# Transformer encoder layer on one core: the order of the ramp in front of the first Strassen products

## The chip, the cores and the metric

The kernel runs on one core of one Trainium2 chip. The core has five engines with instruction queues of their own: TensorE (PE, matrix products into the PSUM banks), VectorE (DVE), ScalarE (ACT), GpSimd (POOL, here for small fills and for issuing DMAs) and SyncE (SP, which issues most DMAs). Each engine runs its queue in order and waits on semaphores of the others. The metric is the device time of one run in microseconds (us); lower is better.

## What is computed

One layer of a bidirectional encoder with SEQ 1024 tokens and D_MODEL 2048, all in float32. Cut to what matters here:

```python
mod = jax.nn.silu(c) @ w_ada + b_ada
shift, scale, gate = jnp.split(mod, 3, axis=-1)
h = rmsnorm(x, pre_g) * (1.0 + scale[:, None]) + shift[:, None]
proj = h @ w_in                       # 2048 -> 4608
q, k, v, gate_a, u, gate_p = jnp.split(proj, SPLIT_POINTS, axis=-1)
y_a = windowed_gqa(q, k, v, rel_table, sink) * jax.nn.silu(gate_a)
y_p = multiscale_pool(u, w_pool_grp, pool_scale) * jax.nn.silu(gate_p)
g = jax.nn.sigmoid(h @ w_merge + b_merge)          # 2048 -> 4096
merged = g_a * (y_a @ w_br_attn) + g_p * (y_p @ w_br_pool)
out = x + gate[:, None] * rmsnorm(merged @ w_out, post_g)
```

## The kernel before

Every float32 product is made of three products of rounded halves (hi·hi, hi·lo, lo·hi): `split` writes the hi part on ACT and the lo part on DVE. The large products run through a Strassen variant with seven products per pair of 128 output rows (`strassen`; its operands of the tokens are named B11, B21, B12/T3, T2, T4, T1, B22, its accumulators X, Z, V). Seven such products of one pair are 42 matmuls of 128x512 where two groups of token tiles (j = 0, 1) take part.

Before Strassen can start, h must exist, transposed: x is loaded in rows, turned on PE, normalised, scaled and shifted. That stage is called the ramp here; all the rest of the kernel follows it and is not touched by the change but in three places named below. In the ramp:

- The first eight output pairs ("ramp pairs", numbers 0 to 7) are computed in two halves of the contraction, tiles 0 to 3 first (j = 0, 1), with their partial sums parked in DRAM (`ramp_d`). Pairs 0 to 3 run their first half as plain products (`plain_block(i, blk, j)`, 6 matmuls of 128x512 each) on x that is turned but not yet normalised, and only scaled by the modulation's scale (`raw_operands`). Pairs 4 to 7 run their first half as Strassen products on the real h. Then come tiles 4 to 7 for all eight (`SECOND`, in the order 4, 5, 6, 7, 0, 1, 2, 3), adding the parked sums (`load_parts`).
- The norm factor of a token (`rstd`) needs the sum of squares of its whole row (`square_of`, `norm_row`: 32 instructions, half on ACT, half on DVE). `factors` makes rstd, `spread_factors` turns it with a matmul (tile RB) into `rb`, the factors along the free dimension. A plain block is right only after it is multiplied by rb. `put_by(i, blk, known)` takes a block out of PSUM: with known it multiplies by rb and stores to ramp_d; without it, it copies the block to a tile `c` of the pool `ev`. These tiles are multiplied later in place and then stored (`scale_evicted`).
- `row_sums` and its helpers compute scale and shift of the modulation as matmuls with a one-column vector (GEMV) and turn the result into columns `modc` (matmul PM, then DVE). `warm(n)` issues matmuls whose result nobody reads.
- `fill_two` makes the Strassen operands of tiles 0 to 3 from the turned x: it applies shift and scale, forms the sums T3, T2, T4, T1 and splits each into hi and lo. `first_given(n)` prepares the first three weight operands of pair 4, `fill_last` the operand B22.
- The pool `ev` has 9 tiles of 128x512; the pool `big` has 56 slots and hands them out again in the order in which they come free; `xa` has 5 tiles, `wp` holds the weights ("raw" and "wide", 4 tiles).

`keep(...)` fixes the order of an instruction on its engine as it is written; instructions without it (most of `strassen`, and the parts of pairs 4 on) are placed by the scheduler. PE's order in the ramp is thus the written order. In order, the ramp before: pairs 0 and 1 up to all four blocks evicted unscaled (eight tiles of `ev`), pair 2 wholly, `factors`, `spread_factors`, the four scaled evictions of pair 2, pair 3 with the turns of tiles 4 to 7, the shift's GEMV and `fill_two` between its blocks, and the first Strassen pair.

Of the kernel before, what the change touches and what calls it, by code (L numbers as in the profile page):

```python
# [43 lines left out]
def encoder_layer(ctx: ExitStack, tc: tile.TileContext, x, c, table, w_ada, b_ada, pre_g,  # L44
# [320 lines left out]
    rows = ev.tile([P, 512], F32, tag="ev", name="rows")[0:104, 0:P]  # L365
    for r0, src in ((0, c[0]), (16, b_ada[0, 0:D]), (32, b_ada[0, D:2 * D]),
                    (48, pre_g[0]), (64, b_merge[0]), (96, pool_scale[0])):
        n = src.shape[0] // P
        nc.scalar.dma_start(rows[r0:r0 + n, :], src.rearrange("(r p) -> r p", p=P))
# [63 lines left out]
    rb = [slot("rb", F32) for _ in range(2)]  # L433

    def claim_tile(t):
        nc.gpsimd.memset(t[:, 0:1], 0.0)
# [7 lines left out]
    def spread_factors():  # L444
        for s, tag in enumerate(SEEDED):
# [5 lines left out]
            keep(nc.scalar.activation(rb[s], ps, AF.Copy))  # L451
# [196 lines left out]
    def raw_operands(j, s):  # L648

        for kh, name in enumerate(("B11", "B21") if s == 0 else ("B12", "B22")):  # L650
            src, a = xT[2 * j + kh, s], modc[:, 1, kh, j:j + 1]
# [4 lines left out]
    def scale_turned(j):  # L656

        for kh in range(2):
            for s in range(2):
                keep(nc.vector.tensor_tensor(xT[2 * j + kh, s], xT[2 * j + kh, s], rb[s], ALU.mult))  # L660
# [4 lines left out]
    def fill_two(then):  # L665

        b = {j: [[xT[2 * j + kh, s] for s in range(2)] for kh in range(2)] for j in range(2)}
        t2 = {}

        def shifted(kh, s):  # L670
            for j in range(2):
                keep(modulate(nc.scalar, b[j][kh][s], 2 * j + kh))

        shifted(0, 0)
        for j in range(2):
            pin_put("B11", j, b[j][0][0])
        shifted(0, 1)
        shifted(1, 1)
        then(0)
        for j in range(2):  # L680
            t2[j] = rp.tile([P, 512], F32, tag="tf", name=uid("tf"), bufs=2)
            keep(sub(b[j][0][1], b[j][0][1], b[j][0][0]))
            keep(sub(t2[j], b[j][1][1], b[j][0][1]))
            keep(sub(b[j][0][0], t2[j], b[j][0][0]))
            pin_put("T3", j, b[j][0][0])
        then(1)
        for j in range(2):
            pin_put("T2", j, t2[j])
        shifted(1, 0)
        for j in range(2):  # L690
            pin_put("B21", j, b[j][1][0])
        then(2)
        for j in range(2):
            keep(sub(b[j][1][0], b[j][1][0], t2[j]))
            pin_put("T4", j, b[j][1][0])
        for j in range(2):
            pin_put("T1", j, b[j][0][1])

    def fill_last():

        for j in range(2):
            hi, lo = op["B22"][j]
            keep(nc.scalar.activation(hi, xT[2 * j + 1, 1], AF.Copy))
            keep(sub(lo, xT[2 * j + 1, 1], f32(hi)))
# [29 lines left out]
    for j in range(2):  # L734
        claim(j, ("B11", "B21", "B22"))
        right[j] = slot("B12h"), slot("B12l")
        for t in right[j]:
            claim_tile(f32(t))
    for t in rb:
        claim_tile(t)  # L740
# [10 lines left out]
    for j in range(2):  # L751
        claim(j, ("T3", "T2", "T4", "T1"))
    ramp_raws(4, (0, 1))
    ramp_raws(5, (0, 1))
    ada2 = [ada_tile(2, q) for q in range(5)]
    ada2 = [at[:, kk] for at in ada2 for kk in range(2)] + ada_slots(2, range(10, KT))
# [11 lines left out]
    opened, evicted = {}, {}  # L768
# [13 lines left out]
    def put_by(i, blk, known):  # L782

        t = ev.tile([P, 512], F32, tag="ev", name=uid("c"))
        if known:
            keep(nc.vector.tensor_tensor(t, opened.pop((i, blk)), rb[int(blk[1]) - 1], ALU.mult))  # L786
# [19 lines left out]
    for step in g[:4]:  # L806
        step()
        warm(2)
    g[4]()
    turn_part(0, (0, 1), SEEDED)  # L810
    for k in range(2):
        take_turned(0, k, k == 1)
    wide_weights(0, 0)
    warm(4)
    raw_operands(0, 0)
    plain_block(0, "11", 0, "sc")
    plain_block(0, "21", 0, "sc")
    turn_part(1, (0, 1), ("at", "at"))
    for k in range(2):
        take_turned(1, k, k == 1)  # L820
    raw_operands(0, 1)
# [9 lines left out]
    for si in range(4):  # L831
        square_of(si, 0, si % 2 == 1)
    plain_block(1, "11", 0, SEEDED[0])
    plain_block(1, "21", 0, SEEDED[1])
    g = row_sums(scz, scales[1], partial(scale_columns, 1), 2)
    for step in g[:4]:
        step()
        warm(2)
    for si in range(4, 8):
        square_of(si, 0, si % 2 == 1)  # L840
    g[4]()
    warm(4)
    wide_weights(0, 1)
    raw_operands(1, 0)
    plain_block(0, "11", 1)
    put_by(0, "11", False)
    plain_block(0, "21", 1)
    put_by(0, "21", False)
    raw_operands(1, 1)
    wide_weights(1, 1)  # L850
    plain_block(0, "12", 1)
    put_by(0, "12", False)
    norm_row(0)
    plain_block(0, "22", 1)
    put_by(0, "22", False)
    wide_weights(2, 0)
    plain_block(1, "11", 1)
    put_by(1, "11", False)
    norm_row(1)
    plain_block(1, "21", 1)  # L860
    put_by(1, "21", False)
    for n, blk in enumerate(("12", "22")):
        plain_block(1, blk, 0, "mm")
        plain_block(1, blk, 1)
        put_by(1, blk, False)
        norm_row(2 + n)
    wide_weights(2, 1)
    for n, blk in enumerate(BLOCKS):
# [1042 lines left out]
```

## Time and profile before

| | |
|---|---|
| median of 3 runs | 2143.91 us (2141.66 to 2144.96) |
| profiled execution: its time / its span | 2146.2 us / 2144.4 us |
| PE busy | 2086.1 us (97%) |
| DVE busy | 1556.2 us (73%) |
| ACT busy | 1117.0 us (52%) |
| DMA, mean over the span | 222 GB/s |
| granted TensorE clock, mean | 0.992 |

The profile comes from one execution on the chip. "Busy" counts the time with an instruction of that engine under way; an idle stretch is put down to what ended it. A row of the timeline gives start and length in us, the engine, the line of the kernel, the operation, output<-input and, in brackets, how long the engine had been idle and who released it. PE issues matmuls back to back at shorter intervals than the length of one, so a row of 0.39 us is followed by the next after about 0.23 us.

### The profile page before, as it was taken

To read this page: it belongs to the slowest core of one execution; us is meant where nothing else is said; L and a number is where in the kernel's file an instruction comes from. 1 tells how busy PE (TensorE), PEld (TensorE's weight loads), DVE (VectorE), ACT (ScalarE), POOL (GpSimd) and SP (SyncE) were. 2 spreads that over 40 slices of the span, in tenths; PEclk is the share of its full clock that TensorE was granted. 3 is DMA by queue.
4 is the path that set the end of the run, shared out by engine and by line. 5 is a ranking of instruction groups with operands and counts; after the bars stand their busy time and mean duration, and the time that the engine had idled before them with its cause. 6 is when DMAs were issued, how large, how long until landed. Compare 5 with 4: busy or idle time off the path is not lost.

```text
span 2144.4 us, 29159 instructions
## 1 busy us (share of the span) xinstructions
PE 2086.1 (97%) x9573; PEld 1711.1 (80%) x9573; DVE 1556.2 (73%) x2797; ACT 1117.0 (52%) x2126; POOL 44.3 (2%) x146
## 2 busy tenths in 40 slices
PE   7769999999999999999999999999999999999998
PEld 5547878788888888788888888888888788888887
DVE  3478768677556686677777677866956977889667
ACT  3465444444475453565655543433754645667654
POOL 0100000000000000000000000010000000000000
PEclk9889999999999999999999999999999999999999
DMA  9548877788577357754555466765755565696897
GB/s 343 190 148 293 268 267 244 248 279 287 184 230 229 125 195 272 253 171 162 173 186 170 146 213 220 231 221 190 247 166 168 172 197 186 217 320 199 296 330 252
DMA packets 302577, 476.61 MB, mean 222 GB/s; under 512 B 24274, under 2 KB 139066, under 8 KB 302424
## 3 DMA queue, kind: packets, MB, share of 16 engines
q1 hardware_dynamic: 296192, 457.79, 65.1%
q0 software_dynamic: 5008, 14.80, 1.9%
q10 hardware_dynamic: 1224, 2.15, 0.3%
q8 instruction: 75, 1.23, 0.2%
q14 instruction: 78, 0.64, 0.1%
HBM read 346.70 MB, written 130.05 MB: 222 GB/s over the span
## 4 chain that ended last, share of the span: by engine, by line
PE 83%; DMA 5%; DVE 4%; issue 1%; ACT 1%; SPq 0%; DVEq 0%; ACTq 0%; POOL 0%; POOLq 0%
PE Z L237 27%; PE V L237 18%; PE X L237 18%; PE Z L1618 2%; PE Z L1620 2%; PE Z L1619 2%; PE X L1618 1%; PE V L1618 1%; PE V L1620 1%; PE X L1619 1%; PE X L1620 1%; PE V L1619 1%; DMA raw<-in_w_in_dram 1%; DVE wlo L97 1%; PE PT L1328 1%
## 5 line engine op out<-in xcount | busy, mean ns | idle before, releaser
L96 ACT ACTIVATE whi<-raw 128x512 fp32r<-128x512 f32 (+1 forms) x528 | 316.0, 600 | 500.3 <-PE Z L237 252.1
L97 DVE TENSOR_TENSOR wlo<-raw,whi 128x512 fp32r<-128x512 f32 (+1 forms) x528 | 341.3, 651 | 154.2 <-PE Z L237 115.4
L97 DVE TENSOR_TENSOR wlo<-wr,whi 128x512 fp32r<-128x512 f32 x224 | 150.7, 690 | 51.8 <-ACT whi L96 48.6
L96 ACT ACTIVATE whi<-wr 128x512 fp32r<-128x512 f32 x224 | 138.2, 629 | 87.4 <-DVE wlo L97 27.9
L103 DVE TENSOR_TENSOR raw<-raw,raw 128x512 f32<-128x512 f32 x76 | 52.5, 691 | 101.0 <-DMA raw<-in_w_merge_dram 61.8
L237 PE MATMUL V<-T3h,whi 128*128 128x512 f32 x328 | 90.3, 394 | 19.5 <-DVE c L786 17.7
L237 PE MATMUL X<-B11h,whi 128*128 128x512 f32 x328 | 90.1, 392 | 1.6 <-ACT whi L96 1.6
L237 PE MATMUL Z<-T1h,whi 128*128 128x512 f32 x328 | 89.8, 391 | 1.2 <-ACT u L251 1.2
L237 PE MATMUL Z<-B22h,whi 128*128 128x512 f32 x328 | 89.9, 392 | 0.5 <-ACT u L304 0.5
L96 ACT ACTIVATE whi<-ws 128x512 fp32r<-128x512 f32 (+1 forms) x88 | 53.0, 602 | 71.7 <-PE X L237 60.5
L237 PE MATMUL V<-T4l,whi 128*128 128x512 f32 x328 | 89.1, 390 | 0.5 <-DVE T4l L97 0.5
L237 PE MATMUL Z<-T2h,wlo 128*128 128x512 f32 x328 | 88.9, 390 | 0.6 <-DVE wlo L97 0.6
L237 PE MATMUL X<-B11l,whi 128*128 128x512 f32 x328 | 89.5, 391 | 0.0
L237 PE MATMUL X<-B21h,whi 128*128 128x512 f32 x328 | 89.4, 391 | 0.0
L237 PE MATMUL V<-T4h,whi 128*128 128x512 f32 x328 | 89.3, 391 | 0.0
L237 PE MATMUL V<-T3l,whi 128*128 128x512 f32 x328 | 89.3, 391 | 0.0
L237 PE MATMUL X<-B11h,wlo 128*128 128x512 f32 x328 | 89.2, 391 | 0.0
L237 PE MATMUL Z<-T1l,whi 128*128 128x512 f32 x328 | 89.1, 390 | 0.0
L237 PE MATMUL Z<-T2h,whi 128*128 128x512 f32 x328 | 88.9, 390 | 0.1
L237 PE MATMUL Z<-B22l,whi 128*128 128x512 f32 x328 | 88.9, 390 | 0.0
L237 PE MATMUL V<-T3h,wlo 128*128 128x512 f32 x328 | 88.9, 390 | 0.0
L237 PE MATMUL V<-T4h,wlo 128*128 128x512 f32 x328 | 88.9, 390 | 0.0
(395 smaller groups left out, 4932.5 us busy)
## 6 DMA issues: line engine op xcount, KB each, us to landing
part<-part_d SPq DMA_DIRECT2D x136, 256.0 KB, 5.1
ada<-in_w_ada_dram SPq DMA_DIRECT2D x128, 256.0 KB, 5.0
raw<-in_w_merge_dram SPq DMA_DIRECT2D x64, 512.0 KB, 5.3
wr<-ws_dS SPq DMA_DIRECT2D x60, 512.0 KB, 5.2
raw<-in_w_in_dram SPq DMA_DIRECT2D x56, 512.0 KB, 4.3
wr<-in_w_out_dram SPq DMA_DIRECT2D x48, 512.0 KB, 5.5
proj_d<-part SPq DMA_DIRECT2D x68, 256.0 KB, 2.3
sw<-in_w_out_dram SPq DMA_DIRECT2D x64, 256.0 KB, 5.1
```

The costliest lines, as they stand in the source:

```text
L96: ins = (nc.scalar.activation(hi, src, AF.Copy), nc.vector.tensor_tensor(lo, src, f32(hi), ALU.subtract))
L97: nc.vector.tensor_tensor(lo, src, f32(hi), ALU.subtract))
L103: return (eng or nc.vector).tensor_tensor(o, a, b, ALU.add)
L237: nc.tensor.matmul(ps, w_[:, i], op[mov][j][m_], start=fresh and i == 0 and n == 0, stop=i == nj - 1 and n == 2, skip_group_check=True)
L1328: nc.tensor.transpose(pt[:, i * P:(i + 1) * P], p[:, i * P:(i + 1) * P], ident)
L1618: nc.tensor.matmul(pb, hi, w[0], start=first, stop=False, skip_group_check=True)
L1619: nc.tensor.matmul(pb, lo, w[0], start=False, stop=False, skip_group_check=True)
L1620: nc.tensor.matmul(pb, hi, w[1], start=False, stop=last, skip_group_check=True)
```

## The change

All of it lies in the ramp and in the way the parked sums of pairs 0 and 1 are read again.

1. c is loaded a second time, first of all, as a small tile of its own (`crow`, 16x128), and silu(c) comes from that; the other small vectors (`cols`) are turned later (`small_vectors`), by a copy on DVE instead of ACT.
2. The eight blocks of pairs 0 and 1 are stored to ramp_d unscaled, right after their eviction. The multiplication by rb is made when they are loaded as parts in the second half (`scale_parts`, 8 DVE instructions, not fixed in order). `scale_evicted` is gone.
3. `warm` between the GEMV steps is gone (one warm(4) stays). `raw_operands` of j = 0 reads the turned x straight from PSUM (`turned`).
4. Three of pair 2's blocks and the evictions around them move behind `factors` and `spread_factors`; the row squares move ahead.
5. `fill_two` is replaced: scale and rb are applied together to the turned x (`scale_turned`, `scalar_tensor_tensor`), T1 and T4, which need no shift, and all sums are made on unshifted blocks ahead of the shift (`sums_unshifted`, `sums_over`); the shift goes in when B11, T3, T2, B21, B22 are split (`put_shifted`: `Identity` with bias on ACT, `scalar_tensor_tensor` on DVE; for T3 the difference `dif` of two shifts).
6. Both remaining evictions of pair 3 (blocks 12 and 22) come after `fill_shifted`. The bias lines (`fetch_lines`, `bias_rows`) and `nsink_t` move into the Strassen products (side steps 11, 24, 26).
7. rb becomes one tile of `xa` instead of two slots; so tile group 2 of w_ada takes four `xa` tiles and eight slots instead of five and six.

```diff
+    crow = ev.tile([P, 512], F32, tag="ev", name="crow")[0:16, 0:P]
+    keep(nc.scalar.dma_start(crow, c[0].rearrange("(r p) -> r p", p=P)))
...
-    pr = bank(SEEDED[0], "pr")
-    keep(nc.tensor.transpose(pr[:, 0:104], rows, ident[0:104, 0:104]))
-    keep(nc.scalar.activation(sc, pr[:, 0:16], AF.Silu))
-    keep(nc.scalar.activation(scz[:, :, 0], pr[:, 0:16], AF.Silu))
-    keep(nc.scalar.activation(cols, pr[:, 0:104], AF.Copy))
+    pc = bank(SEEDED[1], "pc")
+    keep(nc.tensor.transpose(pc[:, 0:16], crow, ident[0:16, 0:16]))
+    keep(nc.scalar.activation(scz[:, :, 0], pc[:, 0:16], AF.Silu))
+    keep(nc.scalar.activation(sc, pc[:, 0:16], AF.Silu))
...
-    rb = [slot("rb", F32) for _ in range(2)]
+    rb = xa.tile([P, 2, 512], F32, tag="xa", name="rb")
...
+    def scale_turned(kh, s):
+        for j in range(2):
+            keep(nc.vector.scalar_tensor_tensor(block_of(j, kh, s), block_of(j, kh, s), modc[:, 1, kh, j:j + 1],
+                                                rb[:, s], op0=ALU.mult, op1=ALU.mult))
...
-    def fill_two(then):
...
+    def sums_unshifted():
+        scale_turned(0, 0)
+        scale_turned(0, 1)
+        for j in range(2):
+            keep(sub(block_of(j, 0, 1), block_of(j, 0, 1), block_of(j, 0, 0)))
+        for j in range(2):
+            keep(nc.scalar.activation(op["T1"][j][0], block_of(j, 0, 1), AF.Copy))
+        scale_turned(1, 1)
...
+    def put_shifted(name, src_of, shift_of):
+        for j in range(2):
+            keep(nc.scalar.activation(op[name][j][0], src_of(j), AF.Identity, bias=shift_of(j)))
+        for j in range(2):
+            hi, lo = op[name][j]
+            keep(nc.vector.scalar_tensor_tensor(lo, src_of(j), shift_of(j), f32(hi), op0=ALU.add, op1=ALU.subtract))
...
+    def fill_shifted(then):
+        put_shifted("B11", lambda j: block_of(j, 0, 0), shift(0))
+        then(0)
+        dif = xa2.tile([P, 2], F32, name="dif")
+        keep(sub(dif, modc[:, 0, 1, 0:2], modc[:, 0, 0, 0:2]))
+        put_shifted("T3", lambda j: block_of(j, 0, 1), lambda j: dif[:, j:j + 1])
+        then(1)
+        put_shifted("T2", t2.__getitem__, shift(1))
+        put_shifted("B21", lambda j: block_of(j, 1, 0), shift(1))
+        then(2)
...
             keep(nc.scalar.activation(t, opened.pop((i, blk)), AF.Copy))
-            evicted[i, blk] = t
-
-    def scale_evicted(i, blk):
-        t = evicted.pop((i, blk))
-        keep(nc.vector.tensor_tensor(t, t, rb[int(blk[1]) - 1], ALU.mult))
-        nc.gpsimd.dma_start(block(ramp_d[i], 0)(blk), t)
+            nc.gpsimd.dma_start(block(ramp_d[i], 0)(blk), t)
...
-    fill_two(first_given)
+    plain_block(3, "12", 0, "mm")
+    plain_block(3, "12", 1)
+    g[4]()
+    fill_shifted(first_given)
     plain_block(3, "22", 0, "mm")
     plain_block(3, "22", 1)
+    put_by(3, "12", True)
     put_by(3, "22", True)
     fill_last()
...
+    def scale_parts(i):
+        for blk, t in parts[i].items():
+            nc.vector.tensor_tensor(t, t, rb[:, int(blk[1]) - 1], ALU.mult)
...
+        if n < RAMP - 1 and SECOND[n + 1] < 2:
+            at.append((6, partial(scale_parts, SECOND[n + 1])))
```

How the change moves instructions, at three places. In these rows L779 (before) and L799 (after) are the plain blocks' matmuls, L786 / L806 the scaled evictions, and a tile's number tells it from others of its name.

DVE behind the shift's columns, before: from the first operand's lo part to the eviction `c_1069` that frees a PSUM bank. The rows shown are the middle and the end of it (L106 subtractions, L97 lo parts).

```order
L97 TENSOR_TENSOR B11l_207<-xT_184,B11h_206 128x512
L97 TENSOR_TENSOR wlo_1009<-raw_372,whi_1008 128x256
L106 TENSOR_TENSOR xT_178<-xT_178,xT_176 128x512
L106 TENSOR_TENSOR tf_1012<-xT_182,xT_178 128x512
L106 TENSOR_TENSOR xT_176<-tf_1012,xT_176 128x512
L97 TENSOR_TENSOR T3l_341<-xT_176,T3h_340 128x512
L106 TENSOR_TENSOR xT_186<-xT_186,xT_184 128x512
```

```order
L97 TENSOR_TENSOR T4l_365<-xT_0_188,T4h_364 128x512
L97 TENSOR_TENSOR T1l_353<-xT_178,T1h_352 128x512
L97 TENSOR_TENSOR T1l_369<-xT_186,T1h_368 128x512
L786 TENSOR_TENSOR c_1069<-PB_1056,rb_141 128x512
L106 TENSOR_TENSOR B22l_199<-xT_182,B22h_198 128x512
```

The same place on DVE after the change, from the first lo part to the first rows of T2, and the end.

```order
L706 SCALAR_TENSOR_TENSOR B11l_191<-xT_176,modc,B11h_190 128x512
L706 SCALAR_TENSOR_TENSOR B11l_207<-xT_184,modc,B11h_206 128x512
L97 TENSOR_TENSOR wlo_999<-raw_370,whi_998 128x256
L106 TENSOR_TENSOR dif<-modc 128x2
L706 SCALAR_TENSOR_TENSOR T3l_355<-xT_178,dif,T3h_354 128x512
L706 SCALAR_TENSOR_TENSOR T3l_363<-xT_186,dif,T3h_362 128x512
L106 TENSOR_TENSOR ws_1008<-raw_370 128x256
L97 TENSOR_TENSOR wlo_1011<-ws_1008,whi_1010 128x256
```

```order
L103 TENSOR_TENSOR raw_373<-raw_373 128x2x128
L106 TENSOR_TENSOR raw_370<-raw_370 128x2x128
L97 TENSOR_TENSOR wlo_1025<-raw_370,whi_1024 128x256
L806 TENSOR_TENSOR c_1041<-PB_972,rb 128x512
L806 TENSOR_TENSOR c_1044<-PB_1028,rb 128x512
```

The subtractions of token blocks have moved ahead of the shift's columns: between B11l_191 and c_1041 stand 16 instructions on DVE (the two-element dif among them), between B11l_191 and c_1069 before, 30.

POOL's queue. Before, all 16 stores of plain blocks come after rb exists (L787, L795):

```order
L415 MEMSET xT_336 128x1
L627 MEMSET T3h_340 128x1
L627 MEMSET T3l_341 128x1
L787 DMA ramp_d_86<-c_842 128x512
L787 DMA ramp_d_86<-c_845 128x512
L787 DMA ramp_d_86<-c_848 128x512
L787 DMA ramp_d_86<-c_851 128x512
```

After, the eight of pairs 0 and 1 (L810, ramp_d_84 and _85) stand ahead of the fills that claim the next slots, and so among the loads of the second half of x:

```order
L810 DMA ramp_d_84<-c_671 128x512
L810 DMA ramp_d_85<-c_687 128x512
L810 DMA ramp_d_85<-c_696 128x512
L810 DMA ramp_d_85<-c_722 128x512
L810 DMA ramp_d_85<-c_741 128x512
L421 MEMSET xT_324 128x1
L421 MEMSET xT_326 128x1
```

Eight stores of 256 KB have moved ahead on POOL; those of pairs 2 and 3 still come after rb.

DVE in the second half of the ramp pairs, where pair 7 ends and pair 0 begins (raw_1644 and raw_1754 before, raw_1603 and raw_1713 after, are the weights of pair 7 and of pair 0; V, p, u belong to Strassen). Before:

```order
L103 TENSOR_TENSOR u_483_2023<-V_1970,u_483_2023 128x512
L97 TENSOR_TENSOR wlo_2105<-raw_1644,whi_2104 128x256
L103 TENSOR_TENSOR raw_1875<-raw_1875 128x2x128
L97 TENSOR_TENSOR wlo_2119<-raw_1754,whi_2118 128x256
L103 TENSOR_TENSOR p_477_1994<-p_477_1994,u_494_2069 128x512
```

After, with the four multiplications by rb ahead of pair 0's first weights `wlo_2082`:

```order
L103 TENSOR_TENSOR u_474_1982<-V_1929,u_474_1982 128x512
L977 TENSOR_TENSOR part_1985<-part_1985,rb 128x512
L977 TENSOR_TENSOR part_1987<-part_1987,rb 128x512
L977 TENSOR_TENSOR part_1989<-part_1989,rb 128x512
L103 TENSOR_TENSOR p_468_1953<-p_468_1953,u_485_2028 128x512
L977 TENSOR_TENSOR part_1991<-part_1991,rb 128x512
L97 TENSOR_TENSOR wlo_2068<-raw_1603,whi_2067 128x256
L97 TENSOR_TENSOR wlo_2082<-raw_1713,whi_2081 128x256
```

Four instructions on tiles that a DMA has just loaded now stand ahead of two lo parts that PE waits for; the four of pair 1 stand one by one among the rows that follow.

More of the change, by code (lines that the diff above doesn't have):

```diff
@@ L699, in fill_last @@
     def fill_last():
[L701 to L704, printed above, removed]
+        put_shifted("B22", lambda j: block_of(j, 1, 1), shift(1))
     RAMP_ORDER = [COL_K, COL_V, COL_GA, COL_GA + 256, COL_Q, COL_GA + 512, COL_GA + 768, COL_Q + 256]
@@ L981, in encoder_layer @@
         if i == RAMP - 1:
-            at.append((4, lambda: parts.update({SECOND[0]: load_parts(ev, block(ramp_d[SECOND[0]], 0))})))
+            at.append((4, partial(get_parts, SECOND[0], ev)))
         run(ramp_gen((0, 1), i, None, False, given=() if n else given), side, range(7), at)
```

201 lines of the change are left out of this document (96 added, 105 removed).

## The prediction

> **What bounds the kernel now.** I read the page's slices first, then PE's waits, then the ramp by windows.
>
> ```profile
> span 2144.4 us, 29159 instructions
> PE   7769999999999999999999999999999999999998
> PEclk9889999999999999999999999999999999999999
> ```
>
> The granted clock and PE dip only in the first three slices of 54 us. Behind them PE is full, so only time won in the ramp counts, and whatever later stage makes PE wait costs in full. PE's waits in the first 130 us (total, times, longest):
>
> ```profile
> PE V L237 <- DVE c L786: 17.7, 1, 17.7
> PE PB L779 <- DVE wlo L97: 9.3, 2, 9.1
> ```
>
> These two are 27 us, 1.3% of the span. The windows (length, then busy us of PE, PEld, DVE, ACT, POOL, granted clock, DMA share, GB/s):
>
> ```profile
> 67.30:73.00 5.70, 3.88 (x12) 1.72 (x10) 1.57 (x5) 3.09 (x6) 0.69 (x1) 1.00 0.56 182
> 73.00:82.20 9.20, 0.14 (x1) 0.00 (x0) 2.67 (x4) 1.07 (x2) 1.42 (x3) 0.74 0.20 74
> 82.20:87.50 5.30, 5.28 (x16) 4.41 (x17) 2.74 (x5) 1.19 (x3) 1.82 (x4) 0.50 0.26 98
> 103.40:125.68 22.28, 2.97 (x8) 1.85 (x7) 16.45 (x31) 11.79 (x23) 0.00 (x0) 0.61 0.56 180
> ```
>
> After each long wait the clock is halved: 5.3 us at 0.50 behind the first. Three marks of the timeline cut the ramp: RB (the factors are there), the reduction of the shift's sums, the first Z product.
>
> ```profile
> 67.30 1.02 PE L450 MATMUL RB<-diag,ones 128*128 128x512 f32 x2
> 98.90 0.17 DVE L485 TENSOR_REDUCE pm<-PM 128x4 f32<-128x16 f32 x1 [0.21 <-PE PM L483]
> 128.98 0.62 PE L237 MATMUL Z<-T2h,whi 128*128 128x512 f32 x2
> ```
>
> I forecast the time at Z, then what later stages give back.
>
> **Term 1: when RB comes.** In the changed order RB follows one block of pair 2 instead of four, so PE no longer sets it; the last loads and ACT do. c first, no warm matmuls and operands read from PSUM start the first block sooner or, on a cold clock, no sooner; I cost all three at nothing, for PE, which reached pair 2 at 57.16, now gets there at about 45 (7 us of warm matmuls and 5 of waits less, an estimate) and waits for the last weights:
>
> ```profile
> 57.16 0.50 PE L779 MATMUL PB<-B11h,whi 128*128 128x512 f32 x1 [1.21 <-ACT whi L96]
> L801 PE MATMUL WARM<-ident 128*128 128x128 f32 x48 | 8.8, 319 | 0.0
> 39.55 0.38 SPq L725 DMA_DIRECT2D wide<-in_w_in_dram  x1
> xt<-in_x_dram SPq DMA_DIRECT2D x3, 256.0 KB, 5.4
> 40.00:45.00 5.00, 3.71 (x14) 2.27 (x15) 1.92 (x3) 2.94 (x5) 0.00 (x0) 1.00 1.02 379
> L426 ACT ACTIVATE xt<-xt 128x512 f32<-128x512 f32 x16 | 9.9, 623 | 0.1
> L441 ACT ACT_TABLE_LOAD x1 | 1.3, 1283 | 0.0
> L448 DVE TENSOR_SCALAR diag<-ident,rstd 128x128 f32<-128x128 f32 x8 | 1.8, 282 | 4.0 <-PE RB L450 4.0
> ```
>
> The last wide tile is issued at 39.55; x tiles just ahead took 5.4 us to land, and twice the bytes add 0.7, so about 46. The DMA engines are full then (share 1.02), and some five of the moved stores (5 x 0.26 MB) now go out before it: at 379 GB/s 0 to 3.5 us; I take 2, so 48. ACT has that tile's hi part pinned ahead of what remains: hi part, five squares and two evictions at 0.62 (5.0), the table load 1.28, 0.5 for root and reciprocal, the hi part of pair 3 0.4 behind that, then on DVE its lo part 0.6 and four diags (0.9): 48 + 8.7, so **RB at 57**, 10.3 earlier; bounds 54.5 (stores free) to 60 (in full, and ACT late). The Trainium skill ("DMA: Bandwidth & Descriptors", section "Queues, rings and completion order") says that each DMA engine takes turns between its queues by packets, whichever engine issued them. By that rule the stores delay the loads in full, RB comes 1.5 us later than I take, and the sum would be 1.5 more; no row of before has such a store among full loads.
>
> **Term 2: RB to the shift's sums**, 31.6 us before. Out go 9.1 (wlo) and half of 5.3 at half clock (2.6), and RB's and the next block's waits, 1.8:
>
> ```profile
> 69.28 1.12 PE L450 MATMUL RB<-diag,ones 128*128 128x512 f32 x2 [0.97 <-DVE diag L448]
> 71.26 0.50 PE L779 MATMUL PB<-B11h,whi 128*128 128x512 f32 x1 [0.85 <-DVE c L786]
> 77.50 0.69 DVE L786 TENSOR_TENSOR c<-PB,rb 128x512 f32<-128x512 f32 x1 [2.77 <-DMA ramp_d<-c]
> 81.48 0.68 DVE L97 TENSOR_TENSOR wlo<-wide,whi 128x512 fp32r<-128x512 f32 x1
> 97.34 1.09 PE L462 MATMUL XT<-ident,xt 128*128 128x128 f32 x8
> ```
>
> The 77.50 row shows the cause: eight of the nine ev tiles held unscaled blocks, so each eviction waited for the store of the one before, 2.8 us each, with the lo part of the weights queued behind. After, those tiles are stored from 36 us on, and no row has them to wait for. In come three blocks of pair 2, 36 matmuls at 0.226 (8.2; 42 take 9.5 in a full window, below); one turn more ahead of the sums (1.0, the 97.34 row); half clock again, because PE idles some 6 us before RB (2.5, bounds 0 and the 3.9 of a slower start); and 1.5 where the third turn waits for four rows scaled on ACT (0 to 1.9). DVE's new work there (14 scalings and subtractions at about 0.65, 9 us) lies beside 20 us of PE work on pairs 2 and 3, with the PSUM banks freed before and after it; it costs nothing, unless DVE were 6 us late. 31.6 - 13.5 + 8.2 + 1.0 + 2.5 + 1.5 = 31.3; bounds 28 and 34.
>
> **Term 3: sums to Z**, 30.1 us before. V waited for a bank, whose eviction stood on DVE behind all of the fill, and the fill handed each block back and forth:
>
> ```profile
> 105.06 1.22 PE L237 MATMUL X<-B11h,whi 128*128 128x512 f32 x2 [1.61 <-ACT whi L96]
> 111.17 0.63 ACT L96 ACTIVATE T3h<-xT 128x512 fp32r<-128x512 f32 x1 [2.93 <-DVE xT L106]
> 111.89 0.69 DVE L97 TENSOR_TENSOR T3l<-xT,T3h 128x512 fp32r<-128x512 f32 x1 [0.80 <-ACT T3h L96]
> 125.68 0.76 PE L237 MATMUL V<-T3h,whi 128*128 128x512 f32 x1 [17.70 <-DVE c L786]
> 126.24 1.05 PE L947 MATMUL OPEN<-B11h 128*128 128x512 f32 x2
> 17.73 0.75 DVE L654 SCALAR_TENSOR_TENSOR B11l<-xT,modc,B11h 128x512 fp32r<-128x512 f32 x1
> 18.40 0.75 DVE L654 SCALAR_TENSOR_TENSOR B21l<-xT,modc,B21h 128x512 fp32r<-128x512 f32 x1
> ```
>
> After, DVE has from the columns (0.4) to the eviction that frees X's bank: eight lo parts at 0.67 (5.4, from the two starts above), eight small ones for the weights at 0.37 (3.0), the eviction 0.6, the first wait for ACT 0.8 and two more of 0.5: 11.2 (9, with no wait, to 14, with 0.8 at each pair as in the 111.89 row). PE has one block and the OPEN pair meanwhile, then idles some 8 us; X and V then run at half clock at first, 6 x 0.43 and 2.1. 0.4 + 11.2 + 2.6 + 2.1 = 16.3, so **13.8 less**. The wait does not vanish; X has it instead of V.
>
> The Trainium skill ("TensorE: Matmul & The Clock Gate", section "Part 1: The HAM clock gate") puts the half clock after a pause at about 3.4 us of sustained work where the row has 5.3 us. By it each of the two cold starts is up to 0.9 us cheaper and the sum up to 1.8 less.
>
> **Term 4: given back later.** The bias matmul ran in a wait (102.42) and now costs 0.9 on a full PE. The eight scalings come on DVE where pairs 0 and 1 load their parts:
>
> ```profile
> 102.42 1.02 PE L395 MATMUL BIAS<-oh,tab 33*8 33x512 f32 x2
> 205.00:214.50 9.50, 9.50 (x43) 7.88 (x42) 8.00 (x18) 4.67 (x10) 0.00 (x0) 1.00 0.80 251
> 209.30 2.58 SPq L209 DMA_DIRECT2D part<-ramp_d  x4
> part<-ramp_d SPq DMA_DIRECT2D x4, 256.0 KB, 3.7
> 212.37 0.68 DVE L103 TENSOR_TENSOR u<-V,u 128x512 f32<-128x512 f32 x1
> 213.65 0.43 DVE L97 TENSOR_TENSOR wlo<-raw,whi 128x256 fp32r<-128x256 f32 x1
> 214.29 0.62 PE L237 MATMUL X<-B11h,wlo 128*128 128x512 f32 x2
> ```
>
> DVE is busy 8.0 of a pair's 9.5 us and gets 2.4 more. Worse is the place: the four scalings stand between the 212.37 and the 213.65 row, and that lo part has 0.2 us to spare before PE wants it (214.29). The loads go out from 209.3 to 211.9 and take 3.7, so the last is scaled at 216.2 and the lo part is done at 216.9: PE waits 2.7. Pair 1's stand one by one, but its last two loads wait for buffers; I put the same 2.7 there. Term: 0.9 + 5.4 (bounds 0, all hidden, and 10, a full landing for each pair).
>
> **Sum**: -10.3 - 0.3 - 13.8 + 6.3 = -18.1 against the profiled execution's 2146.2 (span 2144.4), which is 2.3 above the median of 2143.91; against the median 2125.8. I forecast **2126 us**.
>
> **Rivals.**
> - *The scalings are free, or the stores delay nothing*: 2.4 us could slip into DVE's gaps if parts land sooner. For: 1.5 us idle per pair; against: the lo part's 0.2 us. Gives 2126 - 5.4 = 2120.6, or 2123 for the stores, both 2118.
> - *The fill stays a hand-to-hand chain, and the factors come late*: 14 instead of 11.2 in term 3 and RB at 60: 2126 + 2.8 + 3 = 2132. For: ACT has 8 shifted hi parts at 0.75 to 0.8 and three small ones, nearly as much as DVE.
> - *Slower, by the parts in the second half*: a scaling holds DVE until its tile has landed, with PE's weights behind it. It decides from a mean wait of 24.4 / 8 = 3.1 us per scaling on: 18.1 + 6.3 = 24.4 is what the rest wins. With 3.7 for each it is 2143.9 - 24.4 + 8 x 3.7 = 2149. Against: four loads are under way together, so one landing serves several.
> - *No change*: the stores' wait and the fill's wait are replaced by others of the same length. It would take a further 18 us of PE idle in a ramp whose queues show none.
>
> **How the numbers follow.** What can be told from no change is about 0.2%, 4.3 us. Forecast 0.51 (own range 2121 to 2131), cheaper 0.25 (2115 to 2121), dearer 0.17 (2131 to 2138), no change 0.04, slower 0.03. The range 2115 to 2138 leaves out the last two and a tail below. Faster 0.93 is the first three; same 0.04 and slower 0.03 are the others.
>
> **What would show it.** Right: RB's first matmul at 55 to 60; no eviction waiting for a store of ramp_d; one PE wait of 7 to 11 us, before X, with the eviction of block 12 as its releaser; Z at 102 to 108; DVE waiting for a DMA at the scalings of the parts, with PE waits of 2 to 3 us there. Wrong: RB later than 62, a new wait in the two blocks behind it, a PE wait behind the first Strassen pair for a late load, or no waits at the scalings.

## The result, and the profile after

The changed kernel takes 2122.39 us (median of 4 runs, 2119.09 to 2123.97) against 2143.09 for the kernel before on the same chip: a ratio of 0.9901, 95% interval 0.9884 to 0.9918, or 20.7 us less. On a second chip it took 2121.93 against 2143.91, 0.9897 (0.9882 to 0.9912). The forecast was 2126, in a range of 2115 to 2138. The profiled execution after took 2119.09 us, the lowest of its four; the one before lay 2.3 us above its median. So the two spans differ by 27.1 us where the medians differ by 20.7; a part of that scatter is traced below.

The page after, the same rows as before (length of the span, then the 40 slices of 53 us each):

```profile
span 2117.3 us, 29060 instructions
PE   7799999999999999999999999999999999999998
PEclk9899999999999999999999999999999999999999
```

One dip fewer: the third slice is full now. PE's waits in the first 130 us (total, times, longest):

```profile
PE X L237 <- DVE c L806: 9.2, 1, 9.2
PE RB L453 <- DVE diag L451: 5.8, 1, 5.8
PE pc L380 <- DMA crow<-in_c_dram: 3.3, 1, 3.3
PE PB L799 <- ACT whi L96: 1.0, 1, 1.0
PE PM L486 <- ACT acc L506: 0.5, 1, 0.5
...
PE XT L465 <- ACT xt L457: 0.2, 1, 0.2
```

The 17.7 us before V and the 9.1 us for the lo part are gone. New are 9.2 us before X and 5.8 us before RB. The three marks, with the rows that set them, from the timeline:

```profile
47.49 0.63 ACT L96 ACTIVATE whi<-wide 128x512 fp32r<-128x512 f32 x1 [3.78 <-DMA wide<-in_w_in_dram]
56.13 3.78 PE L453 MATMUL RB<-diag,ones 128*128 128x512 f32 x4 [5.78 <-DVE diag L451]
86.12 0.18 DVE L488 TENSOR_REDUCE pm<-PM 128x4 f32<-128x16 f32 x1 [5.38 <-PE PM L486]
97.67 1.28 DVE L806 TENSOR_TENSOR c<-PB,rb 128x512 f32<-128x512 f32 x2
98.50 1.19 PE L237 MATMUL X<-B11h,whi 128*128 128x512 f32 x2 [9.19 <-DVE c L806]
103.55 0.62 PE L237 MATMUL Z<-T2h,whi 128*128 128x512 f32 x2
```

RB comes 11.2 us earlier than before, the sums of the shift 12.8, Z 25.4. ACT waits 3.78 us for the last wide tile, and RB follows 8.6 us behind that. DVE reaches the evictions that free X's bank only at 97.67, behind the whole fill. Behind Z the two executions need nearly the same: 2144.4 - 128.98 = 2015.4 us before, 2117.3 - 103.55 = 2013.8 after. The windows (length, busy us of PE, PEld, DVE, ACT, POOL, granted clock, DMA share, GB/s) show both pauses of PE and the clock behind each:

```profile
50.00:55.00 5.00, 0.35 (x2) 0.00 (x0) 2.17 (x9) 4.51 (x10) 1.55 (x12) 0.71 1.05 402
55.00:60.00 5.00, 3.87 (x5) 1.81 (x6) 2.55 (x10) 0.65 (x2) 0.14 (x1) 0.50 1.05 395
90.00:95.00 5.00, 0.00 (x0) 0.00 (x0) 4.47 (x8) 3.40 (x6) 0.00 (x0) 0.81 1.10 356
95.00:100.00 5.00, 1.50 (x4) 1.24 (x5) 4.46 (x10) 1.95 (x4) 1.27 (x3) 0.50 1.10 348
```

### The profile page after: what moved, and what is told of

The parts are those of the page before. It is cut to its first block, busy times and chain, and to the rows that moved or that the text cites. A ratio compares the mean times of both kernels' runs of the same rounds, so it can differ in the third digit from the quotient of the medians.

```text
span 2117.3 us, 29060 instructions
## 1 busy us (share of the span) xinstructions
PE 2080.0 (98%) x9534; PEld 1707.1 (81%) x9534; DVE 1554.3 (73%) x2799; ACT 1113.1 (53%) x2117; POOL 43.8 (2%) x144
## 4 chain that ended last, share of the span: by engine, by line
PE 92%; DMA 4%; DVE 2%; ACT 1%; issue 0%; SPq 0%; ACTq 0%; DVEq 0%; POOL 0%
PE Z L237 30%; PE X L237 20%; PE V L237 20%; PE Z L1645 2%; PE Z L1647 2%; PE Z L1646 2%; PE V L1647 1%; PE X L1647 1%; PE X L1646 1%; PE V L1646 1%; PE X L1645 1%; PE V L1645 1%; PE PB L799 1%; DMA xt<-in_x_dram 1%; PE PT L1355 1%; DMA raw<-in_w_merge_dram 1%
## 5 line engine op out<-in xcount | busy, mean ns | idle before, releaser
L97 DVE TENSOR_TENSOR wlo<-raw,whi 128x512 fp32r<-128x512 f32 (+1 forms) x528 | 340.1, 649 | 155.9 <-PE Z L237 112.5
L97 DVE TENSOR_TENSOR wlo<-wr,whi 128x512 fp32r<-128x512 f32 x224 | 150.5, 688 | 51.1 <-ACT whi L96 48.1
L237 PE MATMUL X<-B21l,whi 128*128 128x512 f32 x328 | 88.9, 390 | 0.0
```

What stands on the lines that cost most here:

```text
L97: nc.vector.tensor_tensor(lo, src, f32(hi), ALU.subtract))
L237: nc.tensor.matmul(ps, w_[:, i], op[mov][j][m_], start=fresh and i == 0 and n == 0, stop=i == nj - 1 and n == 2, skip_group_check=True)
```

## The experiments

The theory: the gain is two stalls taken out of PE's path, the evictions that waited for stores and the fill behind the shift, and nothing else in the change moves the end. The main rivals: the factors' earlier time is what wins; or the scalings on load eat 5 us. Each kernel was timed in 5 rounds beside the kernel before, in three groups, each on one chip. The marks are each kernel's profiled execution, in us; "wide" is the start of ACT's split of the last wide tile where ACT waited for its load.

| kernel | median, us | ratio to before (95%) | wide | RB | sums | Z | span - Z |
|---|---|---|---|---|---|---|---|
| before | 2144.96 / 2143.75 / 2143.91 | 1 | - | 67.30 | 98.90 | 128.98 | 2015.4 |
| changed | 2122.39 | 0.9901 (0.9884-0.9918) | 47.49 | 56.13 | 86.12 | 103.55 | 2013.8 |
| changed, again | 2121.93 | 0.9897 (0.9882-0.9912) | 48.60 | 57.24 | 86.17 | 103.11 | 2014.9 |
| stores alone | 2135.58 | 0.9955 (0.9942-0.9967) | - | 67.13 | 86.06 | 116.39 | 2018.9 |
| fill of before | 2135.52 | 0.9959 (0.9946-0.9972) | 48.15 | 56.78 | 86.08 | 117.21 | 2019.8 |
| c, warm back | 2120.88 | 0.9885 (0.9871-0.9900) | - | 56.52 | 83.47 | 100.34 | 2017.6 |
| no scaling | 2121.74 | 0.9883 (0.9864-0.9901) | 51.21 | 59.84 | 89.32 | 106.53 | 2015.6 |
| stores held | 2122.60 | 0.9894 (0.9879-0.9909) | 46.30 | 54.94 | 87.69 | 105.15 | 2016.4 |
| evictions ahead | 2117.64 | 0.9873 (0.9855-0.9891) | 50.72 | 59.36 | 89.34 | 100.49 | 2017.0 |
| split behind factors | 2115.95 | 0.9867 (0.9853-0.9882) | - | 53.98 | 81.22 | 98.85 | 2015.0 |
| both | 2112.74 | 0.9851 (0.9836-0.9866) | - | 53.75 | 82.41 | 93.57 | 2016.7 |
| three moves | 2110.98 | 0.9849 (0.9832-0.9866) | - | 53.53 | 83.10 | 91.89 | 2017.7 |
| warm at RB | 2120.19 | 0.9893 (0.9877-0.9910) | 47.43 | 56.35 | 83.24 | 100.27 | 2015.1 |
| three moves, warm | 2111.93 | 0.9852 (0.9837-0.9867) | - | 54.10 | 82.39 | 91.19 | 2021.8 |

### The stores alone (kernel before plus parts 2 and 7)

```diff
-            evicted[i, blk] = t
+            nc.gpsimd.dma_start(block(ramp_d[i], 0)(blk), t)
...
-    for blk in BLOCKS:
-        scale_evicted(0, blk)
...
+    def scale_parts(i):
+        for blk, t in parts[i].items():
+            nc.vector.tensor_tensor(t, t, rb[int(blk[1]) - 1], ALU.mult)
```

> The kernel before with one part of the change alone: the eight blocks of pairs 0 and 1 go to DRAM unscaled right after eviction and are multiplied by rb when they are loaded again (rb lies in one tile of xa, as in the changed kernel). Theory: the waits of pair 2's evictions for a free ev tile go away, and with them the 9.1 us that PE waited for the lo part of the weights and half of the 5.3 us at half clock; the scalings in the second half cost about 1 us, as the trace of the changed kernel has it. 2143.1 - 9.1 - 2.6 + 1 = 2132 us, RB still near 67 because PE sets it there. Rival A (the scalings cost the 5.4 us of the prediction): 2137. Rival B (the wait moves to the next load or to the fill): 2143.

Measured: 9.4 us less by the medians, 1.3 us short of the 10.7 of the theory. Rows of its trace, from the timeline and PE's waits:

```profile
67.13 1.88 PE L451 MATMUL RB<-diag,ones 128*128 128x512 f32 x4
86.06 0.17 DVE L486 TENSOR_REDUCE pm<-PM 128x4 f32<-128x16 f32 x1 [0.22 <-PE PM L484]
PE V L237 <- DVE c L785: 18.8, 1, 18.8
116.39 1.05 PE L237 MATMUL Z<-T2h,whi 128*128 128x512 f32 x2
```

RB stands where it stood (67.30 before), yet the sums come at 86.06, where the changed kernel has them too (86.12). Z is 12.6 us earlier and V's wait is still there (18.8 us, 17.7 before). So the store stall is worth 12.6 us at Z, and RB's 11 us earlier in the changed kernel show no gain at the sums: PE does then behind RB what it did before it, and in part at half clock. Behind Z this profile needs 3.5 us more than the one before (2018.9 and 2015.4); 1.4 of it is a wait of PE at the scalings, the rest stays open.

### The fill of before in the changed kernel

```diff
-    fill_shifted(first_given)
+    fill_two(first_given)
...
-    sums_unshifted()
+    scale_turned_before(0)
...
-    sums_over()
+    scale_turned_before(1)
```

> The changed kernel with the fill of before: rb by a multiplication of its own, shift and sums in fill_two behind the columns of the shift. All else as changed. Theory: the fill is worth what the traces show between the sums of the shift and the first Z product, 30.1 us before and 17.4 after, so this costs about 12 us: 2134 us, with one PE wait near 20 us in front of the first or second product. Rival (only the factors' earlier time and the stores count, the fill lies beside other work): 2123.

Measured: 2135.52, 13.1 us above the changed kernel's 2122.39. The wait before X:

```profile
PE X L237 <- DVE c L836: 23.3, 1, 23.3
117.21 0.62 PE L237 MATMUL Z<-T2h,whi 128*128 128x512 f32 x2
```

Up to the sums the two kernels are the same (86.08 and 86.12); then the old fill needs 31.1 us to Z where the new one needs 17.4. The two experiments add up: 12.6 us of stores and 13.7 of the fill are 26.3 at Z, and the whole change has 25.4. For c first, the missing warm matmuls, the order around the factors and the rest of the change, nothing is left as a net; the next kernel shows that two of these work against each other.

### c and the warm matmuls back

```diff
-    crow = ev.tile([P, 512], F32, tag="ev", name="crow")[0:16, 0:P]
...
+    for step in g[:4]:
+        step()
+        warm(2)
...
-    raw_operands(0, 0, True)
+    raw_operands(0, 0)
```

> The changed kernel with c again taken from the small vectors' tile, the warming matmuls back between the column sums, and the first operands read from SBUF again instead of PSUM. Theory (the prediction put all three at nothing, because the last loads set the factors): the first plain block starts within 0.5 us of 17.3, PE comes to pair 2 some 5 us later than 45.7, RB stays at 56 to 58: 2122 to 2124 us. Rival (PE's early start does move RB, as the last row sums stand among the evictions of pair 1 on ACT): RB at 60 or later, 2127.

Measured: 2120.88, not to be told from the changed kernel. The first plain block starts at 18.43, later than the 17.3 that was expected; but the changed kernel itself has 17.33 in one profile and 18.07 in the other. RB stays at 56.52. What differs is the clock: PE idles 2.98 us ahead of RB instead of 5.78, and the window behind has the full clock, where the changed kernel had 0.50:

```profile
56.52 1.98 PE L447 MATMUL RB<-diag,ones 128*128 128x512 f32 x4 [2.98 <-DVE diag L445]
55.00:60.00 5.00, 3.48 (x12) 2.21 (x13) 2.94 (x10) 2.05 (x4) 0.54 (x1) 1.00 1.05 396
83.47 0.17 DVE L482 TENSOR_REDUCE pm<-PM 128x4 f32<-128x16 f32 x1 [5.38 <-PE PM L480]
```

RB to the sums takes 26.95 us instead of 29.99. So, as far as single profiles tell, parts 1 and 3 together cost 3 us at Z, because PE idles longer ahead of RB and loses its clock; the medians show 1.5 with intervals that overlap. With the full clock the sums come at 83.47, 2.6 us ahead of those of the stores alone (86.06): that much the earlier factors bring, and the lost clock takes it away again.

### No scaling

```diff
-        if n < RAMP - 1 and SECOND[n + 1] < 2:
-            at.append((6, partial(scale_parts, SECOND[n + 1])))
```

> The changed kernel without the eight multiplications of the parts of pairs 0 and 1 (that part of the computation is left out: these sums stay unscaled). The prediction put them at 5.4 us: 2117 us. The waits in the trace of the changed kernel (0.2 and 1.1 us) give 1.3 us: 2121. Rival, that they are hidden wholly: 2122.4.

Measured: 2121.74, 0.7 below the changed kernel's 2122.39 and 0.2 below its 2121.93. The four runs lie between 2117.59 and 2124.04, so the timing alone can't tell 1 us from 5; the traces can. The scalings that wait, and PE's one longer wait there, in the changed kernel:

```profile
190.51 0.69 DVE L977 TENSOR_TENSOR part<-part,rb 128x512 f32<-128x512 f32 x1 [0.47 <-DMA part<-ramp_d]
196.11 0.69 DVE L977 TENSOR_TENSOR part<-part,rb 128x512 f32<-128x512 f32 x1 [0.43 <-DMA part<-ramp_d]
202.67 0.69 DVE L977 TENSOR_TENSOR part<-part,rb 128x512 f32<-128x512 f32 x1 [0.47 <-DMA part<-ramp_d]
203.28 0.42 DVE L106 TENSOR_TENSOR raw<-raw 128x256 f32<-128x256 f32 x1
203.79 1.34 ACT L96 ACTIVATE whi<-raw 128x256 fp32r<-128x256 f32 x4 [2.56 <-DVE raw L106]
204.26 0.73 PE L237 MATMUL Z<-T2h,whi 128*128 128x512 f32 x2 [0.91 <-ACT whi L96]
```

DVE does stand and wait for a landing, but three times for less than 0.5 us. The last of these scalings stands ahead of a subtraction of weights (203.28), whose hi part on ACT (203.79) is what PE waits for, 0.9 us once (1.7 there in the second profile of the changed kernel, and 0.2 for a lo part). Between 180 and 230 us PE idles for 0.9 to 1.9 us in each of the twelve profiles with the scalings, and not at all in the two without them, this one and the kernel before. So the price is 0.9 to 1.9 us, and 5.4 is excluded.

### The stores held back

```diff
+    keep(nc.gpsimd.tensor_copy(seen, wide[1, 1][:, 0, 0:1]))
+    for i, blk, t in held:
+        keep(nc.gpsimd.dma_start(block(ramp_d[i], 0)(blk), t))
```

> The changed kernel with the eight unscaled stores held back until the last wide tile of w_in has landed, so that no store goes out beside it (a one-column copy on POOL waits for the tile, the stores stand behind it). It prices the stores among full loads. If they delay the loads by all their bytes (3.5 us), the tile lands at 44.0 instead of 47.5, RB comes at 52.6 and the time is 2119 us; with the 2 us that the prediction took, 45.5, 54.1 and 2120.4; if they are free, 47.5, 56.1 and 2122.4. A wait for one of the nine ev tiles could cost 1 to 3 us behind RB.

Measured: 2122.60, no gain. The issue of the last wide tile and the start of its split in this kernel, DVE's waits from 55 to 90 us, and last the same issue in the changed kernel's first profile:

```profile
40.31 0.38 SPq L745 DMA_DIRECT2D wide<-in_w_in_dram  x1
46.30 0.63 ACT L96 ACTIVATE whi<-wide 128x512 fp32r<-128x512 f32 x1 [1.76 <-DMA wide<-in_w_in_dram]
DVE c L806 <- DMA ramp_d<-c: 9.3, 2, 6.2
38.97 0.38 SPq L745 DMA_DIRECT2D wide<-in_w_in_dram  x1
```

The tile is split at 46.30. In the six profiles that have the stores beside it and let ACT wait, the start is 47.43, 47.49, 48.15, 48.60, 50.72 and 51.21, a mean of 48.9. But the load is not issued at the same time in all of them (38.97 to 40.87). Counted from its issue, the split starts after 6.0 us here, after 8.4 to 8.6 in four of the six and after 9.9 and 10.9 in the other two. So the stores cost 2.4 to 4.9 us there, 3.1 in the mean, more than the 2 us of the prediction; with one profile of the held stores no more can be said. The 1.2 us that RB wins against the first profile are lost behind it, because the evictions of pair 2 again wait for stores (9.3 us on DVE): the very wait that the change removed comes back.

### Three moves that go on from there

Evictions ahead, and the split of the last wide tile behind the factors, each alone and then both. Block 22 is now evicted inside `fill_shifted`, behind its first operand B11; the split stood ahead of the squares of rows 5 to 7:

```diff
+    put_by(3, "12", True)
     g[4]()
-    fill_shifted(first_given)
     plain_block(3, "22", 0, "mm")
     plain_block(3, "22", 1)
-    put_by(3, "12", True)
-    put_by(3, "22", True)
+    fill_shifted(first_given)
...
-    wide_weights(2, 1)
...
     factors()
     plain_block(2, "11", 0, "sc")
+    wide_weights(2, 1)
     plain_block(2, "11", 1)
```

> The changed kernel with the evictions of pair 3's blocks 12 and 22 ahead: 12 before the columns of the shift are reduced (DVE idles 5.4 us there), 22 behind the first operand pair. It takes X's 9.2 us wait away. Theory: X starts at about 89.5 instead of 98.5, and Z is then bound by its weight's hi part at 97.3 instead of 103.55; as DVE stays behind for a few products, 4 to 6 of these 6.2 us are won: 2117 us. Rival (DVE, not the bank, bounds the first products, and the wait only moves to V, Z and the products behind): 2121 to 2122.

> The changed kernel with the split of the last wide tile (pair 2) moved behind the factors on ACT, where it stood ahead of the last three rows' squares and held them for 3.8 us while it waited for the load. Theory: the squares follow the last x tile (about 45 us), RB comes at 51 to 52 instead of 56.1, 3 to 5 us less: 2118.5 us. Rival (the x rows land no sooner than the wide tile, or the stage behind is bound by the loads): RB at 54 or later, 2121 to 2122.

> Both moves at once, the evictions of pair 3 ahead and the split of the last wide tile behind the factors. They lie in different stages, so the gains should add: 2122.4 - 5 - 4 = 2113 us. Rival (the loads of the shift's weights bound the sums once RB is early): no better than the evictions alone, 2117.

Measured: 2117.64, 2115.95 and 2112.74. First the evictions ahead:

```profile
92.19 0.61 PE L237 MATMUL X<-B11h,whi 128*128 128x512 f32 x2
100.49 1.22 PE L237 MATMUL Z<-T2h,whi 128*128 128x512 f32 x2 [2.41 <-ACT whi L96]
```

X waits no more (2.9 us behind the sums instead of 12.4), and Z waits 2.4 us for its weight; from the sums to Z it takes 11.2 us instead of 17.4. Then the split behind the factors:

```profile
53.98 2.26 PE L453 MATMUL RB<-diag,ones 128*128 128x512 f32 x4
```

RB at 53.98 is 2 us later than expected, since the second half of pair 2's first block, which stands ahead of RB on PE, now waits for that split; but RB to the sums (81.22) takes 27.2 us: PE's idle time is 3.5 us, and the clock is halved from 51.3 to 54.7 only. Against 2122.2, the mean of the changed kernel's two medians, the moves win 4.5 and 6.2 alone and 9.4 together: they add but for some 1 us.

The third move makes the first three weight operands of pair 4 ahead of the shift:

```diff
+    first_given(0)
+    first_given(1)
+    given_sums()
     plain_block(3, "12", 0, "mm")
```

> Both moves (evictions of pair 3 ahead, split of the last wide tile behind the factors) and a third: the first three weight operands of pair 4, which need no shift, are summed and split ahead of the shift's columns where DVE idles 4.9 us; only the third's split stays behind the first T3 pair. In the kernel with both moves V waits 1.9 us and Z 3.3 for these operands. Theory: both waits go and Z comes at 89 to 90 instead of 93.57, 3.5 to 4.5 us less than that kernel's 2112.7: 2109 us. Rival (the next operands, B21 and B22, are late instead, DVE being the bound): 2111 to 2113.

```profile
91.89 1.22 PE L237 MATMUL Z<-T2h,whi 128*128 128x512 f32 x2 [2.60 <-ACT Z L287]
91.27 0.58 ACT L287 ACTIVATE Z<-X 128x512 f32<-128x512 f32 x1
```

V's wait of 1.9 us is gone, but Z still waits 2.6: now for the eviction of X, which stands on ACT behind the hi parts of T2, B21 and B22. Z starts 8.8 us behind the sums, 11.2 without the move. 2110.98 is the best kernel of the study; against the changed kernel on its chip (2121.93) it takes 11 us less. Its lead over the two moves, 1.8 us, is within the scatter.

### A warm clock at the factors

```diff
+    warm(28)
     spread_factors()
```

> The changed kernel with 28 warming matmuls (some 0.18 us each, 5 us) in PE's 5.8 us wait ahead of RB. Theory (term 2 of the prediction: 2.5 us at half clock behind that wait): the clock stays at 1.0 behind RB, RB to the shift's sums takes 27 instead of 30.0 us, 2119.5 us. Rival (the half clock is hidden behind ACT and DVE, or the warming itself delays RB): 2122.

```profile
55.00:60.00 5.00, 5.00 (x27) 3.69 (x26) 2.49 (x10) 2.32 (x5) 0.54 (x1) 1.00 1.05 398
```

The clock stays full, RB is hardly delayed (56.35; 8.9 us behind the split, 8.6 without the warming), and the sums follow at 83.24, in 26.89 us instead of the changed kernel's 29.99 and 28.93. The median, 2120.19, is 1.7 below the changed kernel's on the same chip; the intervals overlap, so the timing alone doesn't tell it from nothing.

> The three moves and 20 warming matmuls (3.7 us) in the wait for the last wide tile's split, ahead of RB. Theory: another 2 us less than with the three moves alone, 2107 us. Rival: the warm clock there frees nothing, as loads or ACT bound the stage behind: same as the three moves.

Here the same addition (`warm(20)` ahead of the last split, on top of the three moves) won nothing, 2111.93 against 2110.98. RB to the sums takes 28.3 instead of 29.6, and Z comes 0.7 us earlier, but the part behind Z is 4.1 us longer in this profile. Which of its waits makes that, a part of the kernel that is the same in both, stays open.

### The changed kernel again

> The changed kernel as it is, once more, beside the others on this chip. Theory: the last wide tile lands anywhere from 47.5 to 51.2 us, as in the four profiles of kernels that are the same up to there, and RB, Z and the end follow it: median 2122, and in its profile the time behind Z within 2 us of 2015. Rival (the scatter of its times is made behind the ramp): the landing near 47.5 whatever the time.

The rows of the second profile, and beside them those of the kernel without scalings, which is the same up to there:

```profile
48.60 0.63 ACT L96 ACTIVATE whi<-wide 128x512 fp32r<-128x512 f32 x1 [4.17 <-DMA wide<-in_w_in_dram]
103.11 0.63 PE L237 MATMUL Z<-T2h,whi 128*128 128x512 f32 x2
51.21 0.63 ACT L96 ACTIVATE whi<-wide 128x512 fp32r<-128x512 f32 x1 [7.01 <-DMA wide<-in_w_in_dram]
106.53 0.62 PE L237 MATMUL Z<-T2h,whi 128*128 128x512 f32 x2
```

RB stands 8.6 us behind this start in every one of them. But only RB follows the landing in both. In the second profile of the changed kernel the split starts 1.1 us later than in the first, and nothing of it is left at the sums (86.17 and 86.12), because less of PE's work behind RB falls into the half clock; Z is even 0.4 us earlier, and the time behind it is 2014.9, as expected. With the split at 51.21, 3.7 us later than in the first profile, Z is 3.0 us later and the span 4.8 longer (2117.3 and 2122.1), 1.8 of it behind Z. So the landing of that one load can make part of the kernel's scatter, but the clock can hide it, and the time behind Z scatters by itself. With one profile of the kernel before, the same can't be checked there.

## Why the prediction was right, and where it was not

**The marks.** RB was put at 57; the five profiles with the stores and the split as changed, and no warming, have 56.13, 56.78, 57.24, 59.36 and 59.84, all within its 54.5 to 60. The path was as described: last wide tile, squares, table load, root, diag. Z was put at 104.6; the three profiles with the changed fill and evictions have 103.55, 103.11 and 106.53, a mean of 104.4. The 24.4 us that the first three terms gave were right within the scatter, in part by luck: term 2 was 1.3 to 2.4 us too dear and term 3 0.6 to 1.1 too cheap.

**Term 1.** The landing was put at 48 with 2 us for the stores. The mean start of the split is 48.9, and counted from the load's issue the stores cost 2.4 to 4.9 us, 3.1 in the mean. The Trainium skill's rule ("DMA: Bandwidth & Descriptors", section "Queues, rings and completion order"), by which the stores take their turns among the loads, has the direction right, and the trace agrees with it as far as it goes: the 3.5 us of all their bytes lie inside that range. Four of the six profiles are below it and two above, so the bytes alone don't make the number. c first and the operands from PSUM were put at nothing for PE, and are within the scatter (17.33 and 18.07 for the first block, 17.66 before). The missing warm matmuls were too, rightly for RB; but they are also why PE idled longer, and 3.0 us of half clock follow, which the prediction had in term 2.

**Term 2** came out at 29.99 and 28.93 against 31.3. The 2.5 us for the half clock are 2.0 to 3.1 by the two kernels with a warm clock there; what was too dear is the third turn's wait, put at 1.5, which the trace has at 0.2. That DVE's new work there costs nothing held, though it is eight scalings, eight subtractions and four lo parts where 14 instructions were counted: between RB and the sums PE has no wait over 0.5 us, and that one is for ACT.

**Term 3** was 17.43 and 16.94 against 16.3. X waited 9.2 us (7 to 11 were forecast), for the eviction named. The first X product was 12.4 us behind the sums; 0.4 + 11.2 had been summed. The parts named in the prediction come to 10.8, so the 0.4 for the columns is in its sum twice; without it the term is 15.9.

**Term 4 is the step that failed.** The scalings were put at 2.7 us for each of two pairs, because the lo part behind them (213.65) was taken to have 0.2 us to spare before PE wants it at 214.29, and the last part would be scaled at 216.2. Measured: 0.9 to 1.9 us for both pairs together, and no PE wait at all at pair 0. The landings were nearly right: in the kernel after, the last part of pair 0 is scaled by 192.4, 2.3 us behind the start of X<-B11h,wlo (190.08), where 1.9 had been forecast. Wrong was the matmul with which the lo part was paired. `strassen` splits the first three weights of a pair in the order of their products, B11, T3 (the one that is formed in a tile `ws`) and T2. These are rows of the kernel before:

```profile
209.57 0.43 DVE L97 TENSOR_TENSOR wlo<-raw,whi 128x256 fp32r<-128x256 f32 x1 [0.40 <-PE Z L237]
211.58 0.42 DVE L97 TENSOR_TENSOR wlo<-ws,whi 128x256 fp32r<-128x256 f32 x1
217.01 0.62 PE L237 MATMUL Z<-B22h,wlo 128*128 128x512 f32 x2
218.37 0.62 PE L237 MATMUL Z<-T2h,wlo 128*128 128x512 f32 x2
```

The lo part that PE reads at 214.29 (B11) was made at 209.57, ahead of T3's (211.58) and ahead of the place where the scalings went. The row at 213.65 stands behind T3's: it is T2's, which PE reads at 218.37, and the other lo part behind the scalings (212.97, of pair 7's last product B22) is read at 217.01. They had 4.3 and 3.6 us to spare and not 0.2; with the prediction's own 216.9 for the first of them PE would not have waited. So the two lo parts that stand behind the scalings, shown with the change, are not ones that PE waits for. The kernel after has them for the same two products, and there the scalings eat up the lead of the first without a wait:

```profile
192.33 0.75 DVE L97 TENSOR_TENSOR wlo<-raw,whi 128x256 fp32r<-128x256 f32 x2
192.80 0.74 PE L237 MATMUL Z<-B22h,wlo 128*128 128x512 f32 x2
```

The one wait, 0.9 us at 204.26 in pair 1, comes by another way, the subtraction of weights behind the last scaling. Of the forecast's 3.6 us too many, 3.5 to 4.5 are this term, less small misses on the other side. The bias matmul's 0.9 us wasn't tried by itself.

**The rivals.** "Cheaper" (scalings nearly free, 2120.6) is what happened in the second half, and 2122.4 lies between it and the forecast. "Fill stays a chain" didn't happen: 0.6 us at B11, 0.9 at T3 and two waits of 0.5 are all. "Slower by the parts" needed 3.1 us for each of eight scalings; the longest wait was 0.47. "No change" is out.

**What the prediction did not see**: that RB's own time carries no gain here. It booked 10.3 us there and took them back in term 2 as PE's three blocks behind RB and the half clock, so the sum was right, but as a cause "the factors come earlier" was empty; the kernel with the stores alone has the same sums at 86.06 with RB at 67.13.

## What to carry to other kernels

When work is moved from ahead of a mark to behind it, count PE's idle time and its clock, not the mark: here an RB that came 11 us earlier left the sums where they were, since PE had three blocks behind it and a half clock, and two stalls of 12.6 and 13.7 us at Z, one a ring of store buffers and one a bank freed behind a long queue on DVE, were the whole of it. Price a wait that is added to a queue by the lead of the one instruction that reads the delayed operand: follow the tile to its reader, for the matmul that stands next in time may read another. And after a stall is removed, read the next row of the waits: the two rows left here (X's bank, the split that held the squares) gave another 9 us by moving three lines.

## What the runs showed of the hardware

A pause of PE of 2.98 us ahead of RB left the clock at 1.00 (c and the warm matmuls back); one of 3.04 us (the kernel with both moves) had it at 0.50 behind. But the length of a pause doesn't decide by itself: in the second profile of the changed kernel the clock is at 0.50 from 51.07 on, behind a pause of 1.37 us and ahead of the long one of 5.60, which begins at 51.64. The row behind the pause of 3.04, and three stretches at half clock from their first to their last moment: of that kernel, and of the changed kernel's first and second profile.

```profile
50.72 0.80 PE L800 MATMUL PB<-B11h,whi 128*128 128x512 f32 x1 [3.04 <-ACT whi L96]
50.14:56.96 6.82, 6.24 (x11) 3.46 (x11) 3.70 (x12) 1.65 (x4) 0.00 (x0) 0.50 1.04 401
52.10:62.34 10.24, 6.21 (x11) 3.59 (x12) 3.34 (x12) 5.42 (x11) 0.82 (x8) 0.50 1.06 386
51.07:61.31 10.24, 4.64 (x8) 1.91 (x7) 4.76 (x18) 5.39 (x13) 1.89 (x13) 0.50 1.05 392
```

In all 14 traces the stretches at half clock between 20 and 130 us last 3.41, 6.83, 10.24, 13.65, 17.07 or 23.89 us, whole multiples of 3.41. They don't begin with the pause, so how much work falls into one differs between runs of the same program: behind the start of RB it is 6.2 us in the first profile of the changed kernel (56.13 to 62.34) and 4.1 in the second (57.24 to 61.31). The prediction quoted 3.4 us from the Trainium skill ("TensorE: Matmul & The Clock Gate", section "Part 1: The HAM clock gate") beside a row of 5.3. Neither is a price for every cold start: these two lie above the 3.4, one above and one below the 5.3, so the estimate of up to 0.9 us less for each fails in the first profile and is met in part in the second (half of 5.3 - 4.1, 0.6 us). That section of the Trainium skill also calls the window of the activity free-running; the equal stretches, and a pause of 3 us that halves the clock in one kernel and not in another, agree with it.
